# Layer A attention: the gate's weights in loads of two depths, in a ring of four half buffers

## The chip, the cores and the metric

The kernel runs on one core of a Trainium2 chip. The metric is the device time of one execution in microseconds; several executions are made, and their median counts. A profile comes from one further execution, recorded by the hardware profiler.

The engines are named as in the profile: PE is TensorE's matmul, PEld its weight load, DVE is VectorE, ACT is ScalarE, POOL is GpSimd, and SP is SyncE, which here does nothing but issue DMAs, one after the other. A trailing q (SPq) means the engine's instruction sequencer.

## The reference

A trunk of two decoder layers over 2048 tokens of width 1024. Layer A is what matters here:

```
u    = rmsnorm(h, norm_a_g)
proj = u @ w_in_a                       # q | k | v | forget logits | gate
q, k = rmsnorm(q per head), rmsnorm(k per head)
log_f = log_sigmoid(f_logit + b_forget)
o    = fox_attention(q, k, v, log_f)    # 16 heads of 64, causal softmax
                                        # with cumulative forget bias
h    = h + (o * silu(gate)) @ w_out_a
```

Layer B follows: shared keys and values, a second projection, sliding-window attention with sinks, a second gate and output projection. All arrays are float32.

## The kernel before, in words

Matmuls run on pairs of rounded float32 parts: a high and a low part of each operand, and three products (high by high, high by low, low by high) where one would be written.

Layer A is done in stages: the projections of v, k, q and the forget logits; then `attention_a`; then `out_a`, the output projection. The gate's projection is not done with the others. The normalised input (`ut`) and the gate's split weights (`wg`) are written to memory during the projections, and the gate's 768 matmuls are fed into the attention stage between the attention's own.

The attention loop runs over 16 heads x 4 chunks of 512 queries, and within a chunk over pairs of 128-key blocks: 320 steps. A step computes scores for one pair (`scores`, lines 1000 to 1029: matmuls, exponential on ScalarE, the split into a high part on ScalarE, L1019, and a low part on GpSimd, L1020, the sums on VectorE). Three steps later `values` (L1044) multiplies by v; at the end of a chunk ScalarE copies the result out of PSUM (L1052) and two stores go to memory (L1054, L1055). Ahead of it all `max_pieces` (L955 to L971) works out row maxima 13 steps early and sends them to a row of the query operand (`to_row`, four small DMAs, L576). `load_max` and `load_rest` (L897 to L910) fetch the next head's operands. The values have a single PSUM bank, `pa`; the slot `sq`, out of which results are stored, has two buffers.

`gate()` is a Python generator; `feed(n)` advances it after each step, about 2.25 matmuls a step, with one step of rest behind each finished tile. It walks over 4 chunks of tokens (`ch`), 8 tiles of 128 gate features (`ft`) and 8 depths (`dt`, 128 input features each), three matmuls a depth, 24 a tile, all into one PSUM bank. The moving operands `us` (tags `wh` and `wl`, nine buffers each) are the eight depths of `ut` for one chunk. The weights come through `gate_weights(ft, dt)`, which is called at depths 0 and 4: one buffer of the tag `wr` holds four depths, 512 KB, and the tag has two buffers, handed out in turn. A load is written in the program directly before its first matmul. In the last feature tile of a chunk (`turn`) the next chunk's operands are loaded one depth after the other as the old ones come free, and behind depth 3 the next chunk's first weights are asked for:

```
if turn and i == 2:
    ahead.append(operands(ch + 1, dt))
    if dt == NDT // 2 - 1:
        first = gate_weights(0, 0)
```

The last 48 gate matmuls (`KEPT`, two tiles) are kept for the end of the stage, where the weights come alternately through one buffer of the tag `st` and one of `wr`.

The kernel is written in a framework that follows which tile each instruction reads and writes, adds the waits, and orders the instructions of each engine by a planner with costs of its own. So a DMA may stand earlier in SP's queue than in the program. SP takes its queue strictly in order: a DMA that waits for its buffer holds back all that stands behind it.

Of the kernel before, what the change touches and what calls it, by code (L numbers as in the profile page):

```python
# [13 lines left out]
F32R = mybir.dt.float32r  # L14
# [9 lines left out]
P = 128  # L24
# [3 lines left out]
NDT = D // P  # L28
# [72 lines left out]
def f_(ap):  # L101
    return ap.bitcast(F32)
# [51 lines left out]
class Trunk:  # L154
# [714 lines left out]
    def attention_a(self, op):  # L869


        nc, tc, d = self.nc, self.tc, self.d
        kbt, qbt = self.sb("big", [P, 2, S], F32R), self.sb("big", [P, 2, S], F32R)
        for i in range(2):
# [6 lines left out]
            out=mask_m[:, -P:], in_=mask_m[:, -P:], pattern=[[-1, P]], compare_op=ALU.is_ge,  # L881
# [177 lines left out]
            return p == 2 * units[u][1] + 1  # L1059

        def gate_weights(ft, dt):
            w = self.sb(next(weight_slots), [P, 2, 2, 2, P], F32R)
            nc.sync.dma_start(out=f_(w), in_=d["wg"][ft, :, dt // 2 : dt // 2 + 2])
            return w

        def gate():


            def operands(ch, dt):
                both = [self.sb(t, [P, CH], F32R) for t in ("wh", "wl")]  # L1070
                for k in range(2):
                    nc.sync.dma_start(out=f_(both[k]), in_=d["ut"][ch, k, dt])
                return both

            ahead, first = [operands(0, 0)], gate_weights(0, 0)
            ahead += [operands(0, dt) for dt in range(1, NDT)]
            for ch in range(NCH):
                rows, us, ahead = self.factor_rows(0, ch), ahead, []
                for ft in range(NDT):
                    turn = ft == NDT - 1 and ch + 1 < NCH  # L1080
                    ps = self.ps(gate_bank, [P, CH])
                    for dt in range(NDT):
                        if dt % 4 == 0:
                            w = gate_weights(ft, dt) if ft or dt else first
                        for i, (wk, uk) in enumerate(((0, 0), (0, 1), (1, 0))):
                            nc.tensor.matmul(  # L1086
                                ps, w[:, dt // 2 % 2, wk, dt % 2, :], us[dt][uk],
                                start=(dt == 0 and i == 0), stop=(dt == NDT - 1 and i == 2),
                            )
                            if turn and i == 2:  # L1090
                                ahead.append(operands(ch + 1, dt))
                                if dt == NDT // 2 - 1:
                                    first = gate_weights(0, 0)
                            if dt < NDT - 1 or i < 2:
                                yield
                    g = self.sb("sq", [P, CH])
                    nc.vector.tensor_tensor(g, ps, rows, ALU.mult)
                    nc.scalar.activation(g, g, AF.Tanh, scale=0.5)
                    nc.vector.scalar_tensor_tensor(g, g, 1.0, ps, ALU.add, ALU.mult)
                    nc.sync.dma_start(  # L1100
                        out=d["gt"][ft * P : (ft + 1) * P, ch * CH : (ch + 1) * CH], in_=g
                    )
                    yield
# [33 lines left out]
        yield  # L1137
        pht, plt = self.sb("big", [P, 4, 1024], F32R), self.sb("big", [P, 4, 1024], F32R)
        filler, fed, total = gate(), 0, NCH * NDT * NDT * 3
        gate_bank, weight_slots, rest = "pb", cycle(["wr"]), False  # L1140

        def feed(n, pause=False):

# [42 lines left out]
                op.load(PREP_AT.index(n), ("qn", "wh", "qn", "wl"))  # L1186
                op.prepare(PREP_AT.index(n), nc.gpsimd)
        op.load(2, ("qn", "wh", "qn", "wl"))
        gate_bank, weight_slots = "mx", cycle(["st", "wr"])
        for item in pending:  # L1190
            values(item)
            feed(fed + NDT)
        gate_bank = "pb"
# [478 lines left out]
```

## Time and profile before

| what | us |
|---|---|
| median of 3 runs | 2425.86 |
| lowest and highest | 2424.97, 2427.44 |
| the profiled execution, own time | 2423.77 |
| its span, first to last instruction | 2421.8 |
| gate matmuls, first start to last start | 592.9 to 1444.0 |
| TensorE busy | 2403.3 (99%) |

In a group's row of the profile stand line, engine, operation, the tiles written and read, their shapes, the count; then the busy time, the mean of one in ns; then the idle time of the engine just before them, and what ended it. A row of waits has the total in us, the number of times and the longest. A row of the timeline has the start, the duration, and in brackets the idle time before. A row of DMA issues has the count, the size of one and the median time from issue to landing.

### The profile page before, as it was taken

How to read it: one execution, taken by the hardware profiler on the slowest of the kernel's cores; microseconds unless marked ns; L12 is line 12 of the kernel's file. 1: busy time of each engine (PE TensorE's matmuls, PEld its weight loads, DVE VectorE, ACT ScalarE, POOL GpSimd, SP SyncE). 2: the span in 40 equal slices, each digit the busy share in tenths (PEclk: the TensorE clock that was granted, in tenths of full speed). 3: DMA queues.
4: the chain of work that ended last, by engine and by line, in shares of the span. 5: the costliest groups of instructions: out<-in, count | busy, mean ns of one | idle time of the engine just before them, and what ended most of it. 6: DMA issues, size and time to landing. Idle time of an engine off the chain costs nothing.

```text
span 2421.8 us, 36285 instructions
## 1 busy us (share of the span) xinstructions
PE 2403.3 (99%) x11960; PEld 2026.8 (84%) x11960; DVE 1732.2 (72%) x4086; ACT 1261.2 (52%) x2504; POOL 992.9 (41%) x642
## 2 busy tenths in 40 slices
PE   9999999999999999999999999999999999999999
PEld 7888899987888788888888878888888888888887
DVE  7756567735898888888888866556666643677775
ACT  5433324323878777877877761135323321466664
POOL 0000000011878777777878862200011000388885
PEclk9999999999999999999999999999999999999999
DMA  6656555677654655576466549975434484765552
GB/s 192 201 169 194 153 153 167 197 235 234 179 167 127 202 161 150 149 211 174 131 181 181 172 139 301 300 251 163 134 88 122 140 269 141 236 219 181 183 183 75
DMA packets 356989, 436.04 MB, mean 180 GB/s; under 512 B 65280, under 2 KB 248608, under 8 KB 350624
## 3 DMA queue, kind: packets, MB, share of 16 engines
q1 hardware_dynamic: 356800, 433.71, 59.1%
q8 instruction: 95, 1.56, 0.3%
q14 instruction: 94, 0.77, 0.1%
HBM read 273.69 MB, written 159.79 MB: 179 GB/s over the span
## 4 chain that ended last, share of the span: by engine, by line
PE 92%; DMA 4%; DVE 2%; ACT 1%; issue 1%; POOL 0%; SPq 0%; ACTq 0%; POOLq 0%; DVEq 0%
PE b L779 31%; PE pa L1044 10%; PE pb L1086 7%; PE pb L1500 7%; PE sc L1000 5%; PE sc L1001 5%; PE mx L955 5%; PE b L1271 4%; PE pb L742 3%; PE b L1354 3%; PE pa L1439 2%; PE b L742 2%; DMA wr<-wg 1%; PE fl L359 1%; PE pb L359 1%; PE pa L742 1%
## 5 line engine op out<-in xcount | busy, mean ns | idle before, releaser
L779 PE MATMUL b<-wh,big 128*128 128x512 f32 (+3 forms) x2560 | 771.2, 374 | 0.6 <-ACT wh L502 0.4
L1020 POOL TENSOR_TENSOR big<-st,big 128x1024 fp32r<-128x1024 f32 (+1 forms) x320 | 655.4, 2067 | 240.7 <-ACT big L1019 156.6
L779 PEld LDWEIGHTS b<-wh,big 128*128 128x128 f32 x2560 | 470.6, 188 | 71.8 <-ACT wh L502 1.9
L779 PE MATMUL b<-wl,big 128*128 128x512 f32 (+3 forms) x1280 | 473.5, 370 | 0.5 <-DVE wl L503 0.5
L1029 DVE TENSOR_TENSOR ac<-ac,st 128x512 f32<-128x512 f32 (+3 forms) x576 | 352.3, 612 | 52.5 <-ACT st L1016 27.0
L1016 ACT ACTIVATE st<-sc 128x512 f32<-128x512 f32 (+1 forms) x512 | 273.4, 582 | 119.7 <-PE sc L1001 52.5
L1044 PE MATMUL pa<-big 128*128 128x512 f32 (+3 forms) x1280 | 319.0, 365 | 0.6 <-POOL big L1020 0.6
L1019 ACT CAST big<-st 128x1024 fp32r<-128x1024 f32 (+1 forms) x320 | 295.3, 923 | 8.5
L779 PEld LDWEIGHTS b<-wl,big 128*128 128x128 f32 x1280 | 241.3, 189 | 36.0 <-DVE wl L503 3.6
L1044 PEld LDWEIGHTS pa<-big 128*128 128x128 f32 x1280 | 229.1, 190 | 38.7 <-POOL big L1020 2.0
L968 DVE TENSOR_REDUCE mt<-mx 128x1 f32<-128x384 f32 (+1 forms) x360 | 214.1, 597 | 30.6 <-PE mx L955 28.5
L1000 PE MATMUL sc<-big 128*128 128x512 f32 (+3 forms) x640 | 232.9, 368 | 1.1 <-DVE st L558 1.1
L511 ACT ACTIVATE sq<-b,r 128x512 f32<-128x512 f32 (+2 forms) x128 | 77.7, 607 | 298.6 <-PE b L779 298.5
L1001 PE MATMUL sc<-big 67*128 67x512 f32 (+3 forms) x640 | 229.5, 367 | 0.0
L955 PE MATMUL mx<-big 66*128 66x512 f32 (+2 forms) x600 | 225.0, 380 | 0.2
L1086 PE MATMUL pb<-wh,wr 128*128 128x512 f32 x488 | 177.7, 396 | 4.8 <-DMA wr<-wg 4.7
L513 DVE TENSOR_REDUCE sm<-sq 128x8 f32<-128x512 f32 (+2 forms) x128 | 74.8, 584 | 139.7 <-ACT sq L511 139.5
L879 POOL MEMSET rot<- 128x512 bf16 x1 | 0.5, 524 | 418.2 <-PE pb L359 418.2
L1402 POOL TENSOR_TENSOR big<-big,tri 128x1024 fp32r<-128x1024 f32 x60 | 144.2, 2403 | 59.1 <-DVE big L1399 59.1
L963 DVE CUSTOM_DVE_ANT_0 mx<-mx,rot 128x384 f32<-128x384 f32 (+2 forms) x240 | 146.7, 616 | 18.2 <-PE mx L955 17.4
L1000 PEld LDWEIGHTS sc<-big 128*128 128x128 f32 x640 | 121.6, 190 | 22.8 <-DVE st L558 1.5
L1001 PEld LDWEIGHTS sc<-big 67*128 67x128 f32 x640 | 121.8, 190 | 19.3
(285 smaller groups left out, 4123.3 us busy)
## 6 DMA issues: line engine op xcount, KB each, us to landing
wr<-wg SPq DMA_DIRECT2D x62, 512.0 KB, 4.4
va<-st SPq DMA_DIRECT2D x32, 512.0 KB, 4.7
ka<-st SPq DMA_DIRECT2D x64, 256.0 KB, 3.9
ut<-big SPq DMA_DIRECT2D x16, 1024.0 KB, 7.1
big<-ka SPq DMA_DIRECT2D x16, 1024.0 KB
big<-qa SPq DMA_DIRECT2D x16, 1024.0 KB, 7.6
qb<-st SPq DMA_DIRECT2D x64, 256.0 KB, 3.8
big<-qb SPq DMA_DIRECT2D x16, 1024.0 KB, 7.7
```

The lines of the kernel that those rows point to most:

```text
L779: nc.tensor.matmul(ps[:, :n], u[tb // 4][:, dt, us], W[k][dt], start=(dt == 0 and i == 0), stop=(dt == NDT - 1 and i == 2),)
L955: mm = nc.tensor.matmul(ps, qb[:66, i * P : (i + 1) * P], kb[:66, k0:k1], start=True, stop=True,)
L968: nc.vector.reduce_max(o, ps, axis=AX.X)
L1000: nc.tensor.matmul(o, ka[:, ks], qa[:, qs], start=not (last and n_), stop=False)
L1001: nc.tensor.matmul(o, kb[:, ks], qb[:, qs], start=False, stop=not diag)
L1016: nc.scalar.activation(pf[:, off : off + w], ps[:, :w], AF.Exp, scale=HD**-0.5)
L1019: nc.scalar.copy(ph[:, :tw], pf[:, :tw])
L1020: nc.gpsimd.tensor_tensor(pl[:, :tw], pf[:, :tw], f_(ph[:, :tw]), ALU.subtract)
L1029: nc.vector.tensor_tensor(a_, a_, pf[:, off : off + w], ALU.add)
L1044: nc.tensor.matmul(pv[:, q0 : q0 + w], v[:, k, :], src[:, off : off + w], start=(p == 0 and n_ == 0 and i == 0), stop=(last and n_ == 1 an ...
L1086: nc.tensor.matmul(ps, w[:, dt // 2 % 2, wk, dt % 2, :], us[dt][uk], start=(dt == 0 and i == 0), stop=(dt == NDT - 1 and i == 2),)
L1500: nc.tensor.matmul(ps, yt(i, y, slice(p, p + 1))[:, 0, :], W[nh][p // 4][:, k, p % 4, :], start=(p == 0 and n_ == 0), stop=(p == NDT - 1 a ...
```

## The change

`gate_weights` loads two depths (256 KB) in place of four, into halves of buffers. Two buffers of the tag `wr` are taken once at the start of the attention stage and kept; `halves` hands out their four halves in turn. For the last two tiles it hands out two halves of a fresh `st` buffer, then two of the ring, and so on. Weights are now asked for at every even depth; the next chunk's first four depths are asked for in two loads, behind depth 3 and behind depth 5 of the last feature tile.

```
         def gate_weights(ft, dt):
-            w = self.sb(next(weight_slots), [P, 2, 2, 2, P], F32R)
-            nc.sync.dma_start(out=f_(w), in_=d["wg"][ft, :, dt // 2 : dt // 2 + 2])
+            w = next(weight_slots)
+            nc.sync.dma_start(out=f_(w), in_=d["wg"][ft, :, dt // 2])
             return w
+
+        def halves(ring, spare=None):
+            while True:
+                if spare:
+                    w = self.sb(spare, [P, 2, 2, 2, P], F32R)
+                    yield from (w[:, n] for n in range(2))
+                w = next(ring)
+                yield from (w[:, n] for n in range(2))
...
-            ahead, first = [operands(0, 0)], gate_weights(0, 0)
+            ahead, first = [operands(0, 0)], [gate_weights(0, 0), gate_weights(0, 2)]
...
-                        if dt % 4 == 0:
-                            w = gate_weights(ft, dt) if ft or dt else first
+                        if dt % 2 == 0:
+                            w = gate_weights(ft, dt) if ft or dt > 2 else first[dt // 2]
...
-                                ps, w[:, dt // 2 % 2, wk, dt % 2, :], us[dt][uk],
+                                ps, w[:, wk, dt % 2, :], us[dt][uk],
...
                                 if dt == NDT // 2 - 1:
-                                    first = gate_weights(0, 0)
+                                    first = [gate_weights(0, 0)]
+                                elif dt == NDT - 3:
+                                    first.append(gate_weights(0, 2))
...
-        gate_bank, weight_slots, rest = "pb", cycle(["wr"]), False
+        ring = cycle([self.sb("wr", [P, 2, 2, 2, P], F32R) for _ in range(2)])
+        gate_bank, weight_slots, rest = "pb", halves(ring), False
...
-        gate_bank, weight_slots = "mx", cycle(["st", "wr"])
+        gate_bank, weight_slots = "mx", halves(ring, "st")
```

## The prediction

> **What bounds the kernel now.** I read the page first (span, the gate's group, the times to landing), then the attention stage as one window, then who waited for whom on the weight-load side, the matmul side and the DMA queue, then each wait in order of time.
>
> ```profile
> span 2421.8 us, 36285 instructions
> PE 2403.3 (99%) x11960; PEld 2026.8 (84%) x11960; DVE 1732.2 (72%) x4086; ACT 1261.2 (52%) x2504; POOL 992.9 (41%) x642
> L1086 PE MATMUL pb<-wh,wr 128*128 128x512 f32 x488 | 177.7, 396 | 4.8 <-DMA wr<-wg 4.7
> wr<-wg SPq DMA_DIRECT2D x62, 512.0 KB, 4.4
> ka<-st SPq DMA_DIRECT2D x64, 256.0 KB, 3.9
> wh<-ut SPq DMA_DIRECT2D x32, 256.0 KB, 4.6
> wl<-ut SPq DMA_DIRECT2D x32, 256.0 KB, 3.5
> ```
>
> TensorE is busy in 99% of the span. The gate's matmuls are a small share of it, but in the groups shown on the page they are the ones that wait for a transfer. The windows of the stage (one of them, and the sum of all from 590 to 1446 us):
>
> ```profile
> core 0: us, PE busy (x) PEld busy (x) DVE busy (x) ACT busy (x) POOL busy (x), PEclk, DMA share, GB/s
> 800.00:900.00 100.00, 98.60 (x480) 81.53 (x479) 87.89 (x194) 79.03 (x125) 77.64 (x38) 1.00 0.62 179
> sum 856.00, PE 848.98 PEld 702.54 DVE 742.42 ACT 673.01 POOL 667.46; mean PE 94.33 PEld 78.06 DVE 82.49 ACT 74.78 POOL 74.16
> ```
>
> TensorE has 848.98 of 856.00 us, at full clock; VectorE, the next, has 742.42. A wait taken from TensorE should therefore shorten the stage nearly in full. The waits on TensorE's two sides in that window (total, times, longest):
>
> ```profile
> PEld L1010 <- issue: 10.5, 64, 0.2
> PEld pb L1086 <- DMA wr<-wg: 7.6, 8, 1.8
> PEld mx L955 <- DVE mt L968: 2.8, 12, 0.4
> PEld pa L1044 <- POOL big L1020: 2.0, 4, 0.8
> PE pb L1086 <- DMA wr<-wg: 4.7, 6, 1.4
> ```
>
> The first row is 64 short pauses at the mask matmuls. The largest true wait is that for the gate's weights: 7.6 us in eight places. That is all the change can take away directly, 0.31% of the run.
>
> **Where the eight come from.** The weight loads that waited, two that follow one of them, the matmul before the first, and the DMA queue's issues beside two:
>
> ```profile
> 802.04 0.19 PEld L1086 LDWEIGHTS pb<-wh,wr 128*128 128x128 f32 x1 [1.55 <-DMA wr<-wg]
> 932.85 0.19 PEld L1086 LDWEIGHTS pb<-wh,wr 128*128 128x128 f32 x1 [0.44 <-DMA wr<-wg]
> 1029.20 0.19 PEld L1086 LDWEIGHTS pb<-wh,wr 128*128 128x128 f32 x1 [0.87 <-DMA wr<-wg]
> 1087.89 0.19 PEld L1086 LDWEIGHTS pb<-wh,wr 128*128 128x128 f32 x1 [0.25 <-DMA wr<-wg]
> 1246.27 0.19 PEld L1086 LDWEIGHTS pb<-wh,wr 128*128 128x128 f32 x1 [0.72 <-DMA wr<-wg]
> 1258.84 0.19 PEld L1086 LDWEIGHTS pb<-wh,wr 128*128 128x128 f32 x1 [1.16 <-DMA wr<-wg]
> 1304.35 0.19 PEld L1086 LDWEIGHTS pb<-wh,wr 128*128 128x128 f32 x1 [0.77 <-DMA wr<-wg]
> 1358.64 0.19 PEld L1086 LDWEIGHTS pb<-wh,wr 128*128 128x128 f32 x1 [1.82 <-DMA wr<-wg]
> 1358.75 0.19 PEld L1086 LDWEIGHTS pb<-wl,wr 128*128 128x128 f32 x1
> 1358.98 0.42 PEld L1086 LDWEIGHTS pb<-wh,wr 128*128 128x128 f32 x2
> 796.53 0.40 PE L1086 MATMUL pb<-wh,wr 128*128 128x512 f32 x1
> 797.62 0.53 SPq L1063 DMA_DIRECT2D wr<-wg  x1
> 1298.99 0.59 SPq L1055 DMA_DIRECT2D oc<-sq  x1
> 1299.67 1.03 SPq L1063 DMA_DIRECT2D wr<-wg  x2
> 1352.93 1.04 SPq L1063 DMA_DIRECT2D wr<-wg  x2
> ```
>
> They are of two kinds. *Turns*: in the last feature tile of a chunk (three times) the code asks for the next chunk's first weights before it asks for this tile's second half. With two buffers the second half then has to wait for the buffer of the first half of the same tile. At 796.53 the last matmul of that first half starts, at 797.62 the load goes out, 4.4 us later the weight load at 802.04 begins after 1.55 us of idling. The waits at 1029.20 (0.87) and 1258.84 (1.16) are the same place in the other two turns. Together 3.58 us. *Late queue*: the other five (0.44, 0.25, 0.72, 0.77, 1.82, together 4.00 us). At 1299.67 and 1352.93 two gate loads leave together, the first right behind an output's store (1298.99): the earlier load was overdue because the in-order queue of SP stood before that store.
>
> **The change part by part.**
>
> *Bytes, matmuls, PSUM:* the same bytes, 768 gate matmuls and banks. Nothing.
>
> *Turns.* I follow the ring's four halves A to D through the last feature tile: its depths 0, 2 take A, B; the next chunk's first pair takes C; depth 4 takes D; the next chunk's second pair takes A; depth 6 takes B. Depth 4 comes into a half that has been free for the whole of the first half tile, so the 3.58 us should go. What is late next: depth 6, whose half B is left six matmuls before its use, and in the next chunk depth 4, which takes C when the first pair has left it, also six matmuls before. How long six matmuls are:
>
> ```profile
> L1086 PE MATMUL pb<-wh,wr x488: 387/393/504, 592.9 to 1444.0; 128*128 128x512 f32 x163
> PEld pa L1044: 0.2, 1
> L1063 SPq DMA_DIRECT2D wr<-wg x62: 319/430/2677, 509.1 to 1430.0; - x62
> L1086 PEldq EVENT_SEMAPHORE  x19: 51/51/51, 702.7 to 1436.5; - x19
> SPq L1054 <- ACT sq L1052: 106.0, 39, 7.5
> SPq L1063 <- PE mx L955: 62.5, 25, 10.4
> SPq L1063 <- PE pb L1086: 21.3, 7, 8.3
> POOL big L1020 <- PE pa L1044: 5.7, 7, 3.1
> ```
>
> The 768 lie between 592.9 and 1444.0 us, 1.11 us apart on the mean since other matmuls stand between: six are 6.6 us, and 1.4 us if they follow each other at the 0.23 us between 1358.75 and 1358.98. A 256 KB transfer lands in 3.5 to 4.6 us. So the six short places cost between nothing (6.6 above 4.6) and 6 x 3.2 = 19 us. The places of today with no lead at all lost 0.87 to 1.55 us each, and the (also leadless) second load of each next chunk does not stand among the eight. I take 0.5 us for the six together.
>
> *Late queue.* In steady state a load may start when the half used four loads before is left, 18 matmuls (20 us) ahead, in place of 12 (13 us); the half also lands a little sooner (3.5 to 4.6 against 4.4 us). The worst overdue load cost 1.82 us, less than the 6.6 us gained, so I take all 4.00 us as gone; the other end is that none of it goes, since the issue order and not the buffer was at fault in the pairs.
>
> *What a vanished wait is worth.* After a wait the next weight load follows 0.11 us later, where 0.23 is usual (1358.64, 1358.75, 1358.98): 0.12 us of each wait is given back already, and a usual gap of 0.04 (0.23 less 0.19) is in it too. 7.6 less 8 x 0.16 is 6.3 us. The matmul side says 4.7. I take the middle, 5.5.
>
> *SP's queue.* 64 further issues at the median 430 ns are 27.5 us of queue time, spread over 851 us. Queued behind a gate load that waits for its half are the stores of the head's output (L1054, L1055), the row of maxima, and the next head's operands; the output's slot is what ScalarE's copy L1052 needs, and the values' matmuls need that copy. Today SP stands 83.8 us before gate loads (62.5 and 21.3, the two largest rows), while stores themselves wait 106.0 us for ScalarE: the queue is mostly waiting, so the issues fit into its idle time. TensorE waited once, 0.2 us, for L1052. I take 0; bounds are minus 2 (the longer lead means shorter stands at the queue's head) and 27.5 if every issue reached TensorE.
>
> *TensorE's queue.* 64 more landings to wait for: today 19 of them stand as semaphore instructions of their own, 51 ns each, in the sequencer, which runs ahead of the matmuls; no wait of TensorE above is put down to them. At most 64 more are 3.3 us. I take 0.
>
> *Dependence by halves.* That a store into one half is held only by the readers of that half can be seen in a ring of the same make: the weights' low parts are written by GpSimd into quarters of one tile (L1020), and it waited only seven times, 5.7 us, for the matmuls that read them.
>
> The sum: -5.5 + 0.5 = -5.0 us. Against the profiled execution's own 2423.77 us (1.97 of it outside the span) that is 2418.8; that execution lies 2.09 below the median, 2425.86. Against the median: **2420.9 us**.
>
> [...]
>
> **The rivals.**
>
> *Within 0.2% (2425 us or so):* only the turns are cured. For it: the pairs at 1299.67 and 1352.93 went late by their place in the queue, which the same planner sets again. Then 3.58 less 3 x 0.16 is 3.1 saved, less 0.5 to 2 for the short places: 1 to 2.6 us, 2423.3 to 2424.8. This holds also if dependences don't go by halves: then each load waits as before and the time stays 2425.9.
>
> *Slower:* the queue of SP at the end of each head's chunk. There are 64 such ends with their copy L1052. If each gate load blocks the stores behind it and a third of the 27.5 us passes through the copy to the single bank of the values, that is +9.2; with half of the 5.5 kept, 2432.3. It decides from 5.0 + 4.9 = 9.9 us, 0.15 us for each of the 64 ends. Against it: the row of 0.2 us. For it: stores already stand 106 us.
>
> *Faster by more:* the earlier release moves other loads and stores forward too. The waits of TensorE on VectorE and GpSimd above are 4.8; with the whole 7.6 and most of them gone, 2415.
>
> **How the numbers follow.** 0.2% is 4.9 us, about what a measurement of this kernel tells from no change. My sum lies at that edge. Forecast case (4.9 to 7.6 saved) 0.38, more than that 0.08; within 0.2%, with half cured or a planner's shift that eats it, 0.38; slower 0.16. So faster 0.46, same 0.38, slower 0.16. Range 2415 to 2430: the low end from the third rival, the high end from the slower one short of its full price. The forecast case alone is 2418.3 to 2421.
>
> **What would show it.** Right: the gate's weights issued 128 times at 256 KB (124 into wr, 4 into st); TensorE's wait on it from 7.6 to about 0.5 us; no wait at the three turns; SP's stand before L1063 shorter for each load; the stage's end some 5 us earlier, everything after it as long as before. Wrong: waits on wr<-wg at depth 6 of a turn or depth 4 after it; ACT L1052 waiting for stores by several us and L1044 behind it; or a stage equally long with the 5 us turned up as waits on VectorE.

## The result, and the profile after

The kernel after takes **2432.78 us** (median of 8 runs, 2427.88 to 2437.91) against 2424.43 (8 runs, 2422.50 to 2427.44) for the kernel before: ratio 1.003, 95% interval 1.0021 to 1.0039, 8.35 us slower. That is a small effect, 0.3%, but the interval lies clear of 1. The profiled execution took 2434.55 us with a span of 2432.8, 11.0 more than before's span. Followed along the same instructions, the two traces are 0.6 us apart at 590 us, 8.4 at 1409 and about 11 from 1636 us to the end. So nearly all of it arises in the attention stage and at the start of the output projection behind it.

From the page of the kernel after (span, engines, the gate's group, its loads with count, size and median time to landing):

```profile
span 2432.8 us, 36388 instructions
PE 2407.4 (99%) x11960; PEld 2028.6 (83%) x11960; DVE 1730.8 (71%) x4086; ACT 1261.5 (52%) x2504; POOL 993.3 (41%) x642
L1094 PE MATMUL pb<-wh,wr 128*128 128x512 f32 x488 | 178.7, 397 | 9.9 <-DMA wr<-wg 9.8
wr<-wg SPq DMA_DIRECT2D x124, 256.0 KB, 4.1
```

The edit did what it says: 124 loads of 256 KB in place of 62 of 512 KB. But the matmul side now waits 9.8 us for them, not 4.7. And half the bytes land in 4.1 us against 4.4. Who waited on the weight-load side, 590 to 1460 us (total us, times, longest):

```profile
PEld pb L1094 <- DMA wr<-wg: 14.2, 11, 2.3
PEld L1010 <- issue: 10.4, 64, 0.2
PEld b L1282 <- DVE sq L1109: 2.3, 1, 2.3
PEld mx L955 <- DVE m L963: 2.1, 7, 0.4
PEld mx L955 <- DVE mt L968: 2.0, 9, 0.3
PEld pa L1044 <- POOL big L1020: 1.7, 3, 0.8
```

The wait to be removed went from 7.6 us in 8 places to 14.2 in 11: +6.6. The output projection's first wait (L1282, on the gate's last result) went from 1.3 to 2.3: +1.0. The other rows shown are as before or smaller. Seven of the eleven in the timeline of the weight loads:

```profile
1057.40 0.19 PEld L1094 LDWEIGHTS pb<-wh,wr 128*128 128x128 f32 x1 [1.80 <-DMA wr<-wg]
1148.65 0.19 PEld L1094 LDWEIGHTS pb<-wh,wr 128*128 128x128 f32 x1 [1.96 <-DMA wr<-wg]
1254.71 0.19 PEld L1094 LDWEIGHTS pb<-wh,wr 128*128 128x128 f32 x1 [1.75 <-DMA wr<-wg]
1260.60 0.19 PEld L1094 LDWEIGHTS pb<-wh,wr 128*128 128x128 f32 x1 [1.08 <-DMA wr<-wg]
1285.85 0.19 PEld L1094 LDWEIGHTS pb<-wh,wr 128*128 128x128 f32 x1 [2.32 <-DMA wr<-wg]
1311.00 0.19 PEld L1094 LDWEIGHTS pb<-wh,wr 128*128 128x128 f32 x1 [1.21 <-DMA wr<-wg]
1366.42 0.19 PEld L1094 LDWEIGHTS pb<-wh,wr 128*128 128x128 f32 x1 [1.95 <-DMA wr<-wg]
```

And what SP issued ahead of four of them, in the timeline of the DMA queue (start, duration, line, count in a row):

```profile
1049.84 0.67 SPq L1054 DMA_DIRECT2D om<-sq  x1
1051.31 0.47 SPq L1055 DMA_DIRECT2D oc<-sq  x1
1053.07 2.15 SPq L1063 DMA_DIRECT2D wr<-wg  x4
...
1279.65 0.53 SPq L1063 DMA_DIRECT2D wr<-wg  x1
...
1306.70 0.59 SPq L1055 DMA_DIRECT2D oc<-sq  x1
1307.39 1.97 SPq L1063 DMA_DIRECT2D wr<-wg  x4
...
1353.56 6.39 SPq L576 DMA_DIRECT2D big<-m  x8
1360.06 0.54 SPq L1054 DMA_DIRECT2D om<-sq  x1
...
1361.28 0.47 SPq L1055 DMA_DIRECT2D oc<-sq  x1
1361.80 2.03 SPq L1063 DMA_DIRECT2D wr<-wg  x4
```

Read a pair of rows together: four loads leave in a row at 1307.39, right behind an output's stores, and the weight load that needs the first begins at 1311.00, 3.6 us later. At 1361.80 the same, 4.6 us before 1366.42, behind eight issues of row maxima (6.39 us) and the stores. Before, two loads left at these two places (1299.67, 1352.93). The half that the first of the four takes had been left at 1283.7 and at 1336.2, over 20 us before: these loads didn't wait for a buffer, they stood late in the queue. At 1053.07 it is different: SP stood 1.2 us before the first of the four, until the gate's matmuls had left its half.

Which depths the waits are at can be counted off, since the gate's weight loads come in the order of the program. Before, all 7.6 us are at depths 0 and 4, the only ones with a load. After, depths 0 and 4 wait 9.1 us in six places, and depths 2 and 6, which now have loads of their own, 5.1 us in five. So most of the growth of 6.6 us is at the loads that the change added.

Where the rest of the 11.0 us is, the windows show (TensorE's granted clock stands behind POOL's column):

```profile
1276.00:1286.00 10.00, 8.12 (x44) 6.63 (x43) 8.16 (x20) 5.21 (x9) 6.18 (x5) 1.00 0.86 277
1286.70:1290.10 3.40, 3.40 (x10) 2.73 (x10) 0.56 (x1) 2.72 (x5) 0.00 (x0) 0.50 0.49 101
1290.10:1300.00 9.90, 9.90 (x51) 8.25 (x50) 8.75 (x18) 7.63 (x13) 7.85 (x4) 1.00 0.58 161
```

Right behind the longest wait (1285.85, 2.32 us) the clock is 0.50 for 3.4 us, and TensorE does 10 matmuls in it, where 51 take 9.90 us next. At a clock of 0.50 these 3.4 us lose 1.7, an estimate from that clock. A second such stretch begins at 1457.3, behind an idle time of 2.30 us of the weight loads (the row of L1282); before's trace has none in the stage. So the main parts of the 11.0 us are 6.6 of longer waits for weights, 3.4 of half clock and 1.0 at L1282. That they add up to 11.0 exactly is chance: 0.6 was there before the stage, and on the matmul side the waits for weights grew by 5.1 only (9.8 less 4.7).

### The profile page after: what moved, and what is told of

It reads as the page before. It is cut to its first block, busy times and chain, and to the rows that moved or that the text cites. A ratio compares the mean times of both kernels' runs of the same rounds, so it can differ in the third digit from the quotient of the medians.

```text
span 2432.8 us, 36388 instructions
## 1 busy us (share of the span) xinstructions
PE 2407.4 (99%) x11960; PEld 2028.6 (83%) x11960; DVE 1730.8 (71%) x4086; ACT 1261.5 (52%) x2504; POOL 993.3 (41%) x642
## 4 chain that ended last, share of the span: by engine, by line
PE 91%; DMA 4%; DVE 2%; ACT 1%; issue 1%; SPq 0%; POOL 0%; ACTq 0%; DVEq 0%; POOLq 0%
PE b L779 31%; PE pa L1044 9%; PE pb L1511 7%; PE pb L1094 7%; PE b L1282 5%; PE sc L1000 5%; PE sc L1001 5%; PE mx L955 5%; PE pb L742 3%; PE b L742 3%; PE b L1365 2%; PE pa L1450 2%; DMA wr<-wg 2%; PE fl L359 1%; PE pb L359 1%; PE pa L359 1%
## 5 line engine op out<-in xcount | busy, mean ns | idle before, releaser
L1044 PE MATMUL pa<-big 128*128 128x512 f32 (+3 forms) x1280 | 318.6, 365 | 0.8 <-POOL big L1020 0.6
L1044 PEld LDWEIGHTS pa<-big 128*128 128x128 f32 x1280 | 229.4, 190 | 39.3 <-POOL big L1020 1.7
L1282 PE MATMUL b<-big 128*128 128x512 f32 x576 | 137.5, 393 | 1.9 <-DVE sq L1109 1.9
```

Of the source, the lines that this page charges most:

```text
L1044: nc.tensor.matmul(pv[:, q0 : q0 + w], v[:, k, :], src[:, off : off + w], start=(p == 0 and n_ == 0 and i == 0), stop=(last and n_ == 1 an ...
L1282: nc.tensor.matmul(bank[tb][nh], op.y(s_)[:, k, tb * P : (tb + 1) * P], op.W[p_][:, j, nh * CH : (nh + 1) * CH], start=(p_ == 0 and i == 0 ...
```

## The experiments

The theories that the expectations name by letters: A, the order of the loads at the turns; B, the loads stand late in SP's queue, behind stores; C, the number and size of the DMAs; D, keeping the buffers for the stage; E, the 64 further issues. All were timed in five rounds against the kernel before. "Gate waits" are those of the weight-load side for the gate's weights in the stage (7.6 before, 14.2 after; all for `wr`, but for the 4.4 of e10).

| run | us | ratio to before, 95% | gate waits |
|---|---|---|---|
| e1 turn order | 2431.37 | 1.0021 (1.0013 to 1.0030) | 12.4 |
| e2 asked early | 2426.11 | 1.0002 (0.9993 to 1.0011) | 0 |
| e3 split in place | 2425.54 | 0.9995 (0.9987 to 1.0004) | 8.3 |
| e4 kept whole | 2425.62 | 1.0000 (0.9991 to 1.0008) | 6.3 |
| e5 before, early | 2420.37 | 0.9973 (0.9963 to 0.9983) | 0 |
| e6 pairs | 2425.90 | 1.0002 (0.9994 to 1.0011) | 5.9 |
| e7 one ahead | 2421.90 | 0.9987 (0.9977 to 0.9996) | 3.3 |
| e8 three ahead | 2423.17 | 0.9988 (0.9979 to 0.9997) | 1.5 |
| e9 early, split | 2419.95 | 0.9979 (0.9970 to 0.9987) | 0 |
| e10 GpSimd's queue | 2427.68 | 1.0009 (1.0000 to 1.0017) | 4.4 (`wr`: 0) |
| e11 ScalarE's queue | 2427.82 | 1.0007 (0.9996 to 1.0017) | 0 |

**e1, the turns in natural order.** The kernel after; the next chunk's first two loads are both asked for behind the last depth, after all loads of their own tile.

```
                                 ahead.append(operands(ch + 1, dt))
-                                if dt == NDT // 2 - 1:
-                                    first = [gate_weights(0, 0)]
-                                elif dt == NDT - 3:
-                                    first.append(gate_weights(0, 2))
+                                if dt == NDT - 1:
+                                    first = [gate_weights(0, 0), gate_weights(0, 2)]
```

> The changed kernel with one edit: in the last feature tile of a chunk the next chunk's first pair is asked for behind the tile's own last load, so that no half is handed out of turn. Theory A (turns): the out-of-turn asking leaves depth 4 of the next chunk and depth 6 of the turn only six matmuls; their waits in the changed kernel are 0.58, 1.80, 1.09, 0.17 and 2.32 us, 5.96 of 14.2 us. With the edit these go: 14.2 falls to about 8.3 us of weight-load waits, and the time by 5 to 6 us or more (a clock dip less), to about 2426 us. Theory B (queue): what counts is the place in SP's queue; the turns are late for the same reason as the others, and asking later in the program makes the first pair of each chunk late in turn: waits stay at 12 to 16 us, time 2430 to 2434 us.

It stays at 2431.37 us. The rows of its waits need care, and so does the timeline:

```profile
PEld pb L1094 <- DMA wr<-wg: 7.8, 7, 1.7
PEld pb L1094 <- issue: 2.6, 1, 2.6
...
PEld pb L1094 <- DVE ac L1029: 2.0, 1, 2.0
```

```profile
1050.97 2.55 SPq L1063 DMA_DIRECT2D wr<-wg  x4
...
1057.36 0.19 PEld L1094 LDWEIGHTS pb<-wh,wr 128*128 128x128 f32 x1 [2.56 <-issue]
```

The waits put down to "issue" and to VectorE stand at gate weight loads whose transfers landed at that moment (1057.3 and 1272.9), so the gate waits are 7.8 + 2.6 + 2.0 = 12.4 us. The order at the turns is worth 2 of after's 14.2 at most: A doesn't carry the loss.

**e2, the same loads asked for two loads early.** The kernel after; every load stands 12 matmuls ahead of its first use in the program, in order of use.

```
+            todo = iter([(f, t) for _ in range(NCH) for f in range(NDT) for t in range(0, NDT, 2)])
+            asked = []
+            def ask():
+                at = next(todo, None)
+                if at:
+                    asked.append(gate_weights(*at))
...
                         if dt % 2 == 0:
-                            w = gate_weights(ft, dt) if ft or dt > 2 else first[dt // 2]
+                            w = asked.pop(0)
+                            ask()
```

> The changed kernel with one edit: each load is written in the program two loads (12 matmuls) before its first matmul, in place of directly before it, always in the order of use. Theory B (queue): a load goes late because its place in SP's order follows its place in the program, behind stores that wait; earlier in the program, nearly all waits on the gate's weights vanish, 14.2 us to under 2 us, and the time falls to 2418 to 2422 us. Theory A (turns) alone: about 6 of the 14.2 us go, 8 stay, about 2426 us. Theory C (cost of the further DMAs themselves: 64 more issues, transfers under contention): no change in time beyond 2 us, 2430 to 2434 us.

All gate waits are gone: same ring, same 124 loads, only their place in the program moved. That is what B says, and it takes about 6.7 us off after's time (2432.78 less 2426.11; each against its own runs of before, 1.0030 to 1.0002). The time that B expected wasn't reached. In the waits the largest rows behind the mask's pauses are now:

```profile
PEld mx L955 <- DVE mt L968: 3.9, 13, 0.9
PEld pa L1044 <- POOL big L1020: 3.3, 6, 1.1
PEld b L1289 <- DVE sq L1116: 3.0, 1, 3.0
...
PEld mx L955 <- issue: 2.0, 1, 2.0
```

The last is at 1031.42 us, where a head's row maxima need query rows whose load (L899) left at 1023.35, behind operands of a turn, and landed at 1031.4, 8.0 us later. A stretch at clock 0.50 follows it at 1032.3.

**e3, before's loads split in place.** Each 512 KB load of the kernel before becomes two of 256 KB, written where the one stood.

```
-            nc.sync.dma_start(out=f_(w), in_=d["wg"][ft, :, dt // 2 : dt // 2 + 2])
+            for n in range(2):
+                nc.sync.dma_start(out=f_(w[:, n]), in_=d["wg"][ft, :, dt // 2 + n])
```

> The kernel before with one edit: each 512 KB load is issued as two loads of 256 KB, one after the other at the old place, into the two halves of the old buffer; two buffers in turn as before. Theory C (cost of the further DMAs): slower than before by most of the 8 us, 2430 to 2433 us. Theories A and B (places and halves, not the number of DMAs): within 2 us of before, 2422 to 2427 us, waits on the gate's weights 6 to 9 us.

No difference in time, and the gate waits are 8.3 us (before: 7.6):

```profile
PEld pb L1087 <- DMA wr<-wg: 8.3, 10, 2.0
```

Twice the DMAs at half the size cost nothing that can be measured here (by the interval at most 1.0 us, 0.04%): C falls.

**e5, before's whole loads asked for one load early.** e2's edit on the kernel before: one buffer, which is again 12 matmuls ahead.

```
-                            w = gate_weights(ft, dt) if ft or dt else first
+                            w = asked.pop(0)
+                            ask()
```

> The kernel before (whole loads of four depths, two buffers) with one edit: each load is written in the program one load (12 matmuls) before its first matmul, always in the order of use. Theory B: the waits on the gate's weights go from 7.6 us to under 2 us and the time falls by 5 to 6 us, to 2418 to 2420 us: then the place in the program is what matters and not the halves. Theory A: only the three turns' 3.6 us go, about 2421 us. Theory C: as A.

The gate waits are gone and the time is 2420.37 us, faster than both kernels. With the buffers of before the waits could be removed: the buffers were enough.

**e4, whole buffers kept for the stage.** The kernel before, with the two `wr` buffers taken once, as after does, and still filled by 512 KB loads.

```
-            w = self.sb(next(weight_slots), [P, 2, 2, 2, P], F32R)
+            w = next(weight_slots)
...
+        ring = cycle([self.sb("wr", [P, 2, 2, 2, P], F32R) for _ in range(2)])
```

> The kernel before with one edit: the two whole buffers are taken once and kept for the stage, and handed out in turn; loads of four depths at the old places. Theory B (place in SP's queue): the place is unchanged, so are the waits (7 to 9 us) and the time, 2423 to 2427 us. Rival D (keeping the buffers is what costs, since a kept buffer is followed by its readers and not by its release): slower by several us, 2429 to 2433 us.

2425.62 us against 2425.55 for before in the same rounds. Keeping the buffers does nothing that can be measured: D falls. (The gate waits, 6.3 us, are a little under the 7 to 9 expected; so are e6's below.)

**e6, halves asked for in pairs.** The kernel after, with both halves of four depths asked for at depths 0 and 4, where before asked for its whole buffer, and the next chunk's first pair behind depth 3.

```
                         if dt % 2 == 0:
-                            w = gate_weights(ft, dt) if ft or dt > 2 else first[dt // 2]
+                            if dt % 4 == 0:
+                                pair = (
+                                    [gate_weights(ft, dt), gate_weights(ft, dt + 2)]
+                                    if ft or dt else first
+                                )
+                            w = pair[dt // 2 % 2]
```

> The changed kernel with one edit: the halves are asked for in pairs, at depths 0 and 4 and behind depth 3 of a turn, which is where the kernel before asks for its whole loads; ring of halves and 256 KB as changed. Theory B: half of the changed kernel's loads, those of depths 2 and 6, stand six matmuls later in the program than before; with the pairs back at the old places the waits on the gate's weights fall from 14 us to 7 to 9 us, and the time to 2423 to 2428 us. Theory C (further DMAs) or D (ring of halves itself): the waits stay at 12 us or more, 2430 to 2434 us.

The time is back at before's (2425.90 against 2425.55), the waits too:

```profile
PEld pb L1099 <- DMA wr<-wg: 5.9, 7, 1.9
```

Ring, halves and number of loads are after's. What differs from after is only that the second half of each pair is asked for six matmuls sooner. So the loss of the change is that: splitting the load moved the request for depths 2 and 6 six matmuls later in the program. It fits the count by depths above: 5.1 of the 14.2 us are at these two.

**e7 and e8, one and three loads early.** e2 with the request 6 and 18 matmuls ahead in place of 12, by one `ask()` less or one more before the loop:

```
             ahead = [operands(0, 0)]
             ask()
             ask()      # left out in e7
+            ask()      # added in e8
```

> The changed kernel with each load asked for one load (6 matmuls, 6.6 us on the mean) before its first matmul, in the order of use. Theory B: between the changed kernel (no lead in the program, 14.2 us of waits) and two loads of lead (no waits): the single waits were 0.2 to 2.3 us, so 6.6 us should do away with nearly all: under 2 us of waits, time as with two loads, 2423 to 2428 us. If waits of 5 us and more are left, the loads go late by far more than their waits show.

> The changed kernel with each load asked for three loads (18 matmuls) before its first matmul, all that four halves allow. Theory B: waits on the gate's weights stay at zero as with two loads of lead; the time tells whether a longer lead costs: each load then asks for the half that has just been left, so SP stands at its head more often than with two. By the waits alone 2420 to 2426 us, as with two; above 2428 us if SP's stands then delay operands and stores.

One ahead leaves 3.3 us of gate waits in four places and is faster than before, 2421.90 us; three ahead leaves one wait of 1.5, at 1439.9 us in the last two tiles, and takes 2423.17. So e7 has more waits and less time than expected (under 2 us; 2423 to 2428). The waits fall with the distance, 14.2, 3.3, 0; the time doesn't follow them to the end.

**e9, e5 with each buffer filled by two loads.** e3's edit on e5.

```
             w = self.sb(next(weight_slots), [P, 2, 2, 2, P], F32R)
-            nc.sync.dma_start(out=f_(w), in_=d["wg"][ft, :, dt // 2 : dt // 2 + 2])
+            for n in range(2):
+                nc.sync.dma_start(out=f_(w[:, n]), in_=d["wg"][ft, :, dt // 2 + n])
```

> The kernel before with whole buffers asked for one buffer early (2420.4 us, no waits on the gate's weights), and each buffer now filled by two loads of 256 KB, one after the other. It tells what the changed kernel asked early by two halves (2426.1 us, no such waits either) still loses. Theory E (64 more issues in SP's queue delay what stands behind them, the query rows at a turn among it): near 2425 us. Theory F (not the number of loads but the order the planner makes of finer asking): near 2420.4 us, within 1.5 us.

2419.95 us, no gate waits; e5 and e9 overlap in their ratios. The 64 further issues cost nothing that can be measured, also where nothing hides behind a wait for weights: E falls.

**e10 and e11, other queues.** The kernel after with the loads issued by GpSimd (e10) or ScalarE (e11), at after's place in the program.

```
-            nc.sync.dma_start(out=f_(w), in_=d["wg"][ft, :, dt // 2])
+            nc.gpsimd.dma_start(out=f_(w), in_=d["wg"][ft, :, dt // 2])   # e11: nc.scalar
```

> The changed kernel with one edit: the gate's loads are issued by GpSimd's queue in place of SP's; places in the program, halves and sizes as changed. Theory B in its narrow form (it is the stores that stand waiting at the head of SP's queue that make the loads late): no load stands behind a store any more, the waits of TensorE on the gate's weights fall from 14.2 us to under 4 us; the time to 2420 to 2426 us if GpSimd's own work (86 to 88% busy in the densest window) bears 120 issues, more if L1020 goes late. Broad form (any in-order queue that the planner fills by program place makes them late): waits of 8 us and more stay, now behind L1020, time 2430 us and above.

> The same with ScalarE's queue. ScalarE is on the way of each step (exponential, split), so a load that waits for its half holds the attention itself. Narrow form of B: waits on the gate's weights under 4 us, but what is saved is lost to ScalarE standing before loads: 2425 to 2435 us. Broad form: waits of 8 us and more and 2432 us and above.

In both no weight load in the stage waits for `wr`. That is the narrow test of B: same requests, same program places, another queue, and the 14.2 us of waits for `wr` are gone. So what stood ahead of them in SP's queue made the loads late. That it was the stores alone isn't shown: at 1353.56 eight rows of maxima (6.39 us) stood there too. In e10 one wait of 4.4 us for the gate's weights came anew, at the buffer `st`, so its sum misses the "under 4 us" of the narrow form by a little. The time didn't fall below before's. The likely reason, which no run isolates, is that the issuing now stands in an engine that works: in e10 GpSimd spends about 69 us on it (124 issues at a median of 559 ns), and the low parts come later. Two rows of the waits that grew, and the window behind the second:

```profile
PEld pa L1044 <- POOL big L1020: 5.6, 7, 1.3
PEld mx L1094 <- DMA st<-wg: 4.4, 1, 4.4
```

```profile
1436.00:1440.00 4.00, 3.91 (x9) 3.13 (x10) 2.03 (x2) 0.00 (x0) 0.00 (x0) 0.50 1.01 376
```

The 4.4 us end at 1436.09, in the last two tiles. The clock is 0.50 there from 1435.0 to 1441.9, beginning within the wait (0.88 on the mean of 1432 to 1436, 0.77 of 1440 to 1444). In e11 the wait of L1044 for GpSimd is 6.4 us (2.0 before), one of 2.26 us among them at 1430.8.

A load landed no faster from another queue: medians of 4.5 us from GpSimd's and from ScalarE's, 4.1 in the kernel after. And what e10 saved was not the time to issue, a median of 559 ns on GpSimd against 394 on SP in the kernel after: it was the standing behind others in SP's queue, the 14.2 us for `wr`.

## Why the prediction was wrong

The prediction said 2420.9 us, range 2415 to 2430; it came to 2432.78, slower in place of faster and outside the range. The step that failed is *Late queue*, and the short places of *Turns* after it.

*Late queue* (4.00 us, taken as all gone; measured 8.84 at seven places). The step set the gain in lead, 12 to 18 matmuls, against the worst overdue wait. That gain is there on the average, and not where it counted. A lead is here the time from a load's issue to its first matmul, a wait included, worked out from the two traces for all loads but those of the turns, of a chunk's first tile and of the last two tiles of the stage. The median lead rose from 14.2 to 18.6 us, but 6 of 92 loads have under 5 us in place of 2 of 46. The waits there are at loads of that kind, and at 1148.65, whose load left among three in a row (1141.71), 5.0 us before it was needed, and took 6.9 us to land. The buffer gave permission to leave earlier; the place in SP's queue didn't allow it. The prediction named this end itself ("the issue order and not the buffer was at fault in the pairs") and then went by the mean. It also didn't see that a load written directly before its first matmul is, for depths 2 and 6, written six matmuls later than the whole load was, which e6 shows to be the loss. Asking early takes the leads under 5 us to none (e2, e5, e9), and that is when the waits vanish.

*Turns* (3.58 us, to become 0.5; measured 5.38). Two of the three named waits, 802.04 and 1029.20, are gone as worked out. The third is still there (1260.60, 1.08 us): its half was long free, but its load stood between the operands of the turn and left at 1256.32. Of the six short places three wait: depth 4 of the next chunk at 1057.40 (1.80) and 1285.85 (2.32), depth 6 at 1267.31 (0.17), 4.29 us together. They were named as the next late ones, and mis-sized, 0.5 us for 4.29: the mean distance of six matmuls, 6.6 us, against a landing of 3.5 to 4.6. At 1057.40 the distance was short: its half was left at 1053.0 and the load went out at once, 2.5 us before it was needed. At 1285.85 the distance was there, 7.1 us from the half's last matmul (1276.4) to the need (1285.85 less the wait of 2.32). But four issues of row maxima stood ahead, the load left at 1279.65, and it took 6.2 us to be there; in the window 1276 to 1286 us above the DMA share is 0.86.

*What a vanished wait is worth* (5.5 us of 7.6): borne out by another edit. e5 removes all of the gate waits and is 5.6 us faster than before in the same rounds (2425.93 less 2420.37). Some of that agreement is luck, since e5's other waits changed too, and 7 of before's 31 executions in these rounds show a mean clock under 1.000.

*SP's queue* and *TensorE's queue* (0 for the 64 issues): held, e3 and e9. But the bound of minus 2, by which SP would stand for less time, points the wrong way. SP's two largest stands before gate loads sum to 83.8 us before and 120.2 after (79.3 and 40.9); a single load's stand is shorter, since there are twice as many. These stands are not the loss: e6 has 122.8 (79.0 and 43.8) at before's time. *Dependence by halves*: held. Outside the turns 25 of the 46 loads at depths 0 and 4 left while the other half of their buffer still had matmuls to come.

*The slower rival* came within 0.5 us of the time (2432.3) by luck, since its mechanism isn't there: stores held back, then the copy L1052, then the values' matmuls. That chain has 0.9 us after, against 0.2:

```profile
PEld pa L1044 <- ACT sq L1052: 0.9, 2, 0.4
```

It went the other way round: what stands ahead in SP's queue, the stores among it, holds the gate's loads back (14.2 us of waits for `wr` in SP's queue, none in e10 and e11).

*Not in the sum at all:* that two stretches of half clock would come behind idle times of 2.32 and 2.30 us (3.4 us of the 11.0, an estimate), and that the sum of the short ends could come out negative. The signs named for a wrong forecast, waits on `wr<-wg` at depth 6 of a turn and depth 4 after it, are the ones that came.

*What stays open:* e2 and e9 both ask 12 matmuls early and neither waits for weights, yet e2 is some 6 us slower. A part is half clock: the granted clock was below 1.000 in 9 of e2's 12 executions, and the three others took 2422.57 to 2425.19 us. Its own wait at 1031.42 is another part; in e9 the same load (L899) left later, at 1028.69, but its matmul stood later too and waited 0.8. SP's stands before gate loads don't order the runs: their two largest rows sum to 93.8 us in e9, 124.2 in e2, 125.7 in e7 and 144.7 in e8, and both e7 and e8 are faster than e2. Which of the shifts in the planner's order makes the rest wasn't tried.

## What to carry to other kernels

In these runs a load left when three things allowed it: its buffer (SP stood 1.2 us for a half before 1053.07), its place in the program (the second half of each pair asked for six matmuls sooner, in e6, took the waits from 14.2 us to 5.9), and what stood ahead of it in SP's queue (from another queue, in e10 and e11, no load in `wr` was waited for). Look for the shortest leads among the waits, not for the mean one, and see which of the three set them: where several loads left in one row right behind a store, finer buffers didn't help here, and writing the request a buffer's length ahead of its use did (0.9973, with the buffers and loads of before). Whoever splits a load that is written directly before its use moves the request of its second part later.

## What the runs showed of the hardware

TensorE's granted clock fell to 0.50 for stretches of 3.4 us. In the kernel after one began 0.8 us behind an idle time of the weight loads of 2.32 us (to 1285.85; 1.88 on the matmul side), and one 1.5 us behind an idle time of 2.30 (to 1455.84; 1.88 on the matmul side); in e2 one began 0.9 us behind an idle time of 2.02 (to 1031.42; 1.61 on the matmul side). In e10 it fell within an idle time of 4.43 us and stayed for 6.8. In the kernel after, the idle times of 1.96 us (to 1148.65) and 1.95 (to 1366.42), 1.5 on the matmul side, had no such stretch behind them, and before's trace, where the weight loads of the stage stood idle for 1.82 us at most, has none. Not every idle time over 2 us brought one: the weight loads of e1 have three, 2.56 us (to 1057.36), 2.04 (to 1273.03) and 2.4 (L1280), and its profiled execution a mean clock of 0.999, where three stretches of 3.4 us would have made it 0.998 (each takes 1.7 us of 2431). So the length of the idle time alone doesn't decide. It is an observation over these traces; no run changed the idle time alone. e2's:

```profile
1032.30:1035.70 3.40, 3.40 (x10) 2.82 (x10) 2.12 (x8) 2.19 (x3) 1.71 (x2) 0.50 0.99 413
```

The mean granted clock of an execution was below 1.000 in 5 of 8 runs of the kernel after, in 11 of 11 of e1 and of e10, in 23 of 92 of the kernel before (7 of 31, 8 of 34 and 8 of 27 in the three sets of rounds), and in none of e5 (7) and e9 (10). So the profiled execution of the kernel after paid for two of its waits twice, 1.7 us each on top by the estimate above, and the kernel's times scatter: the three runs of after at full clock took 2427.88 to 2430.78 us, the five others 2432.46 to 2437.91.

Halving a load from 512 to 256 KB moved its median time to landing from 4.4 to 4.1 us only, in this stage with a DMA share of 0.58 before (590 to 1449 us) and 0.59 after (590 to 1460). Runs with loads of one size differ by more than that: 3.7 us (e1, e6) to 4.4 (e2) at 256 KB. So the two medians show no sure gain.
